# Reordering a one-core decoder layer: a key search shifted by a fifth, and a few sums and stores moved in the MLP

## The chip, the cores and the metric

The kernel runs on one core of one Trainium2 chip. The metric is device time in microseconds (us), and lower is better. A run is one execution; the profile is of one execution more, taken by the hardware profiler.

## The reference

The layer works on x of 1024 rows by 1024 columns in float32. What the change touches is the sparse attention's choice of keys and the MLP:

```python
# sparse attention: for every query, the 256 best causal keys by an indexer's score
score = einsum(relu(q_idx . k_idx), w_idx) * idx_scale      # per query, per key
score = where(key_pos <= query_pos, score, -inf)
_, sel = top_k(score, 256)                                   # ties: the lower key first
...                                                          # 8 heads attend over sel only
# differential attention: 4 heads, softmax(q1 k1) - lambda * softmax(q2 k2), all causal keys
# x = x + rmsnorm(concat(o_A, o_B) @ W_out)
# MLP
u = relu(rmsnorm(x) @ w_up)              # 1024 -> 4096
y = (u * u) @ w_down                     # 4096 -> 1024
x = x + rmsnorm(y)
```

## The kernel before, in words

Rows are handled in blocks of 128. All large products run in float32 halves: each operand is split into a high part (ScalarE copies it rounded) and a low part (VectorE subtracts), and three products stand for one.

**The search.** Blocks 0 and 1 need no choice. For blocks 2 to 7 the kernel finds each query's threshold bit by bit: `topk_round` counts how many scores lie under a trial threshold, 31 rounds, one bit each. The six blocks form two halves, `TBS = ((3, 5, 6), (2, 4, 7))`; in each round the first block of a half is counted on VectorE, the two others on ScalarE, GpSimd compares, and VectorE sets the bit (L535). `seq(gr)` lists a half's steps: a start, 31 rounds, an end, and then for each block `topk_mask1` and `topk_mask2`, which turn the score into an additive mask with a prefix sum over ties (a scan). That makes 39 steps a half and 78 in all. `topk_mask1` takes two tiles from the three buffers with the tag `pt`: `te` (signs and ties) and `tu` (the scan's result). The transposed probabilities of the differential attention, `pthl`, live in the same three buffers. The steps of both halves are merged one to one into `steps`.

**The differential attention** runs 32 units (head, block) and, between their groups, calls `run_steps(share)`, which issues the steps up to that share of the list, and pieces of the remaining projections (`dense`). Here a planner with its own cost estimates puts the instructions of every engine in order. After it, the sparse attention goes through (head, pair of blocks); its units need the masks, the pair (2, 3) first, then (4, 5), then (6, 7). There TensorE's order is written by hand, with the output projection of the other heads as filler.

**The MLP** has the order of all engines written by hand: `do(t, fn)` files a step under a due time, and all steps are issued in order of these times, so that each engine, and SyncE's DMA queue, gets its instructions in that order. The up projection makes 16 passes p of seven products of 12 matmuls (`P1`, `P6`, `P7`, `P5`, `P2`, `P4`, `P3`; a Strassen-like scheme). A pass p needs weights split in four pieces, `w1` to `w4`, of which `w2` and `w3` come from four sums of raw weights (the tile `su`, L1033 to L1036). Products land in PSUM banks, and some banks are used twice: `P7` fills bank `c`, VectorE adds it to `e2` (this is `e3`, L1273), and only then may `P4` go on in `c`. In the same way `a22` (L1279) reads bank `d` ahead of `P3`. The results are written out by `store`: ScalarE rounds (L1296), VectorE subtracts (L1300), four DMAs write to `u_d` (L1302).

The names `U0` and `D0` are due times: in `U0` the first pass starts its second product, at `D0` the down projection starts. The down projection works in units of 42 matmuls (L1427); unit n reads its left operand from `u_d` by two loads (`down_left`, L1421). In a unit, the first product's bank `a` is copied out by ScalarE (L1458) and used again by the fourth product. The raw down weights come by loads at L997, and pairs of them are subtracted on VectorE (`t13`: L1392, L1393) ahead of a split (`wd_y`).

Of the kernel before, what the change touches and what calls it, by code (L numbers as in the profile page):

```python
# [11 lines left out]
F32 = mybir.dt.float32  # L12
# [4 lines left out]
ALU = mybir.AluOpType  # L17
# [4 lines left out]
P = 128  # L22
D = 1024
S = 1024
# [9 lines left out]
MASK = 2.0 ** 100  # L34
# [16 lines left out]
def hybrid_block(ctx, tc, a):  # L51
    nc = tc.nc
    V, A, G, T = nc.vector, nc.scalar, nc.gpsimd, nc.tensor
# [12 lines left out]
    at = ats.enter_context(tc.tile_pool(name="at", bufs=1, side="right"))  # L66
# [264 lines left out]
    for kt in range(KT):  # L331
# [7 lines left out]
        g = g_preT[:, kt:kt + 1]  # L339
# [4 lines left out]
        elif kt % 3 == 0:  # L344
            n = min(3, KT - kt)
# [112 lines left out]
    score = {}  # L458
# [33 lines left out]
    NT = len(TBS[0])  # L492
# [58 lines left out]
    def topk_mask1(gr, j):  # L551
        i = TBS[gr][j]
        n = (i + 1) * P
        sc, thr = score[i], vbits[gr][:, j:j + 1].bitcast(F32)
        se = at.tile([P, 2, S], BF16, tag="pt", bufs=3, name="te")
        s_, e_ = se[:, 0, :n], se[:, 1, :n]
        u_ = at.tile([P, S], F32, tag="pt", bufs=3, name="tu")[:, :n]
        f = cnt("fm")
        A.activation(s_, sc, AF.Sign, bias=thr, scale=-1.0, accum_out=f[:, 0:1])
        V.tensor_scalar(e_, s_, 0.0, None, op0=ALU.is_equal)  # L560
        V.tensor_tensor_scan(u_, e_, e_, 0.0, op0=ALU.add, op1=ALU.max)

        V.tensor_scalar(f[:, 1:2], u_[:, n - 1:], 0.5, TOPK - n / 2, op0=ALU.mult, op1=ALU.add)
        V.scalar_tensor_tensor(f[:, 2:3], f[:, 0:1], 0.5, f[:, 1:2], op0=ALU.mult, op1=ALU.add)
        mk[i] = s_, e_, u_, f

    def topk_mask2(gr, j):
        i = TBS[gr][j]
        n = (i + 1) * P
        s_, e_, u_, f = mk[i]  # L570

        V.scalar_tensor_tensor(u_, s_, 4.0 * S, u_, op0=ALU.mult, op1=ALU.add)
        V.tensor_scalar(score[i], u_, f[:, 2:3], MASK, op0=ALU.is_gt, op1=ALU.mult)

    def seq(gr):
        r = [lambda: topk_start(gr)]
# [12 lines left out]
            idx_unit(i, h0, 1.5)  # L589
    while dense.run:  # L590
        dense.part()
    steps = []
    for k in range(len(seqs[1])):
        steps += seqs[0][k:k + 1] + seqs[1][k:k + 1]

    while dense.left() > after0:
        with tc.issue_after(anchor0[-1].ins):
# [365 lines left out]
    def do(t, fn, *args):  # L963
        todo.append((t, len(todo), fn, args))
# [52 lines left out]
    def up_weights(p, t):  # L1017

        b = wbox[p]
        do(t["ra"], lambda: b.update(ra=raw(a["wu"][2 * p])))  # L1020
        do(t["rb"], lambda: b.update(rb=raw(a["wu"][2 * p + 1])))

        def s_tile():
            if p == 0:
                b["s"] = my.tile([P, 4, 512], F32, tag="su", bufs=1, name="su0")
            else:
                b["s"] = big("hp", [P, 4, 512], "su", F32)

        s = lambda i: b["s"][:, i, :]
        ra = lambda i: b["ra"][:, i * 512:(i + 1) * 512]  # L1030
        rb = lambda i: b["rb"][:, i * 512:(i + 1) * 512]
        do(t["s"], s_tile)
        do(t["s"], lambda: V.tensor_add(s(2), rb(0), rb(1)))  # L1033
        do(t["s"] + 0.01, lambda: V.tensor_sub(s(1), ra(0), rb(0)))
        do(t["s"] + 0.02, lambda: V.tensor_sub(s(0), s(2), ra(0)))  # L1035
        do(t.get("s4", t["s"] + 0.03), lambda: V.tensor_sub(s(3), ra(1), s(0)))  # L1036
        split_at(*t["w1"], b, "w1", whl, lambda: b["ra"])
        split_at(*t["w2"], b, "w2", whl, lambda: b["s"][:, 0:2, :].rearrange("p a b -> p (a b)"))
        split_at(*t["w3"], b, "w3", whl, lambda: b["s"][:, 2:4, :].rearrange("p a b -> p (a b)"))
        split_at(*t["w4"], b, "w4", lambda: wp.tile([P, 2, 512], F32R, tag="g", bufs=1, name="w_a22"), lambda: rb(1))  # L1040
# [153 lines left out]
    U0 = E + 13.0  # L1194
# [29 lines left out]
    def mlp_up(p):  # L1224
        b = ubox[p]
        plain = p // 2 == NCH - 1
        evt = lambda nm: late["up"].tile([P, 512], F32, tag=nm, bufs=1, name=nm)

        def prod(k, o, l, h, first, last):
            do(start[p, k], lambda: up_mm(b[o], p, l, h, first, last))  # L1230

        def ab():
            ab_ = psS("pab")
            b["a"], b["b"] = ab_[:, 0, :], ab_[:, 1, :]

        def c():
            b["c"] = psM("pc")

        def d():
            b["d"] = psM("pd")  # L1240

        do(start[p, "P1"], ab)
        prod("P1", "a", "A11", "B11", True, False)
        prod("P6", "b", "S2", "T2", True, True)
        do(start[p, "P7"], c)
        prod("P7", "c", "S3", "T3", True, False)
        do(start[p, "P5"], d)
        prod("P5", "d", "S1", "T1", True, False)
        prod("P2", "a", "A12", "B21", False, True)
        prod("P3", "d", "S4", "B22", False, True)  # L1250
        prod("P4", "c", "A22", "T4", False, True)

        def u1():
            b["u1"] = late["up"].tile([P, 2, 512], F32, tag="u1", bufs=1, name="u1")

        def u2():
            b["u2"] = late["up"].tile([P, 2, 512], F32, tag="u2", bufs=1, name="u2")


        a11, a12 = (lambda i=i: b["u1"][:, i, :] for i in range(2))  # L1260
        a22, a21 = (lambda i=i: b["u2"][:, i, :] for i in range(2))

        def e1():
            b["e1"] = sp.tile([P, 512], F32, tag="e1", bufs=2, name="e1")
            A.activation(b["e1"], b["a"], AF.Copy)

        def e2():
            b["e2"] = evt("e2")
            V.tensor_add(b["e2"], b["b"], b["e1"])

        def e3():
            b["e3"] = evt("e3")
            V.tensor_add(b["e3"], b["c"], b["e2"])  # L1273

        do(end[p, "P1"] + 0.01, e1)
        do(end[p, "P6"] + 0.02, e2)
        do(end[p, "P7"] + 0.02, e3)
        do(end[p, "P5"], u2)
        do(end[p, "P5"] + 0.02, lambda: V.tensor_add(a22(), b["d"], b["e3"]))  # L1279
        do(end[p, "P5"] + 0.7, lambda: relu2(a22(), a22()))  # L1280
        t11 = max(end[p, "P2"] + 1.05, OPEN + 6.2 if p == 0 else end[p - 1, "P3"] + 3.5)
        do(t11, u1)
        do(t11 + 0.01, lambda: relu2(a11(), b["a"]))
        do(end[p, "P3"] + 0.02, lambda: V.tensor_add(a21(), b["d"], b["e2"]))
        final = p == NP - 1
        do(end[p, "P3"] + (2.9 if final else 1.2), lambda: relu2(a21(), a21()))
        do(end[p, "P4"] + 0.02, lambda: V.tensor_add(a12(), b["c"], b["e2"]))
        do(end[p, "P4"] + (4.2 if final else 0.65), lambda: relu2(a12(), a12()))
        z = end[p, "P3"]

        def store(src, g, th, tl):

            def hi():
                n = src().shape[1]
                b["st", g] = big("hp", [P, 4, n, 2, P], "stg")
                A.activation(b["st", g][:, :, :, 0, :], src().rearrange("p c (q t) -> p q c t", q=4), AF.Copy)  # L1296

            def lo():
                st, n = b["st", g], src().shape[1]
                V.tensor_sub(st[:, :, :, 1, :], src().rearrange("p c (q t) -> p q c t", q=4), st[:, :, :, 0, :].bitcast(F32))  # L1300
                for q in range(4):
                    ld.dma_start(u_d[p // 2, q, :, p % 2, g:g + n], st[:, q].bitcast(F32))  # L1302

            do(th, hi)
            do(tl, lo)

        s = lambda i: b["sd"][:, i, :]
        if plain:
            store(lambda: b["u1"], 0, z + (3.0 if final else -0.85), z + (4.6 if final else 0.6))
            store(lambda: b["u2"], 2, z + (3.6 if final else 2.3), z + (4.9 if final else 3.4))  # L1310
        else:
            store(lambda: b["u1"], 0, z - 0.85, z + 0.6)
            store(lambda: b["u2"][:, 0:1, :], 6, z - 3.0, z - 2.1)

            def sd():
                b["sd"] = big("hp", [P, 4, 512], "sd", F32)
                V.tensor_add(s(0), a21(), a22())

            do(z + 2.9, sd)
            do(z + 3.0, lambda: V.tensor_sub(s(1), s(0), a11()))  # L1320
            do(z + 3.1, lambda: V.tensor_sub(s(2), a11(), a21()))
            do(z + 3.2, lambda: V.tensor_sub(s(3), a12(), s(1)))
            store(lambda: b["sd"][:, 0:2, :], 2, z + 4.2, z + 5.3)
            store(lambda: b["sd"][:, 2:4, :], 4, z + 5.3, z + 6.5)

    for p in range(NP):
        mlp_up(p)
# [2 lines left out]
                   "w3": (end[0, "P2"] + 0.1, E + 13.8), "w4": (E + 4.5, E + 16.6)})  # L1330
    up_weights(1, {"ra": 2, "rb": 24.0, "w1": (4 * M + 4.9, 4 * M + 7), "s": U0 + 7.6, "w2": (U0 + 9.5, U0 + 10.3),
                   "w3": (U0 + 10.8, U0 + 11.6), "w4": (U0 + 13.8, U0 + 14.4)})
    up_weights(2, {"ra": U0 - 5, "rb": U0 + 9, "s": U0 + 17.0, "w1": (U0 + 16.8, U0 + 18.4), "w2": (U0 + 19.3, U0 + 20.5),
                   "w3": (U0 + 24.8, U0 + 26), "w4": (U0 + 27.6, U0 + 28.5)})
    for p in range(3, NP):
        b = t0(p - 1)
# [311 lines left out]
```

## Time and profile before

| | us |
|---|---|
| runs, median of 3 (lowest to highest) | 1376.77 (1376.04 to 1378.45) |
| the profiled execution's own time | 1375.87 |
| its span in the trace | 1374.1 |

| engine | busy us | share of the span |
|---|---|---|
| TensorE matmuls (PE) | 1290.9 | 94% |
| VectorE (DVE) | 1112.7 | 81% |
| ScalarE (ACT) | 750.2 | 55% |
| GpSimd (POOL) | 381.1 | 28% |

The span and the time of the same execution differ by 1.8 us. A share is a mean over stages: the projections up to about 190 us, the differential attention with the search to about 490, the sparse attention to about 650, the output and the up projection to about 1041, the down projection to the end.

### The profile page before, as it was taken

What the parts mean: (1) busy time and instruction counts of PE and PEld (TensorE: products, weight loads), DVE (VectorE), ACT (ScalarE), POOL (GpSimd) and SP (SyncE); (2) the same over time, 40 slices, a digit from 0 to 9 for tenths busy, and PEclk for the clock granted to TensorE, in tenths of its full rate; (3) what the DMA queues carried; (4) which work ended last, traced back from release to release, by engine and by line L of the source; (5) the groups of instructions that cost most, each with busy time, mean ns of one, the idle gap of its engine ahead of it and who ended that gap; (6) DMA issues with size and microseconds to landing.
All of it is one profiled execution on the core that took longest, in us unless ns stands there. A gap on an engine that the chain in (4) does not pass through costs nothing.

```text
span 1374.1 us, 19888 instructions
## 1 busy us (share of the span) xinstructions
PE 1290.9 (94%) x6520; PEld 1086.3 (79%) x6520; DVE 1112.7 (81%) x1984; ACT 750.2 (55%) x1435; POOL 381.1 (28%) x559
## 2 busy tenths in 40 slices
PE   8999989999998789999888899999999999999997
PEld 8988878778887778887666688888887788888886
DVE  5539999999899888887798888888887488878676
ACT  5215559888994468887455567666676312112112
POOL 6366675676575343331220000000000000000012
PEclk9999999999998889999999999999999999999999
DMA  9674464456556365532751766767678676767656
GB/s 358 210 220 126 122 188 127 120 173 183 151 159 173 111 176 143 159 96 93 241 172 48 257 241 236 259 242 261 234 261 296 239 274 213 272 212 267 219 194 215
DMA packets 152263, 272.82 MB, mean 199 GB/s; under 512 B 15328, under 2 KB 83936, under 8 KB 152160
## 3 DMA queue, kind: packets, MB, share of 16 engines
q1 hardware_dynamic: 152160, 271.55, 59.9%
q8 instruction: 52, 0.85, 0.3%
q14 instruction: 51, 0.42, 0.1%
HBM read 172.40 MB, written 99.09 MB: 198 GB/s over the span
## 4 chain that ended last, share of the span: by engine, by line
PE 56%; DVE 19%; ACT 8%; issue 6%; POOL 5%; DMA 5%; SPq 1%; DVEq 0%; POOLq 0%; ACTq 0%
PE qab L1427 10%; PE pab L1050 8%; PE qc L1427 6%; PE qd L1427 6%; PE pc L1050 6%; PE pd L1050 5%; PE pj L168 3%; ACT jk L530 2%; PE v L356 2%; DVE p L627 2%; PE sa L626 2%; PE yb L895 2%; PE si L474 2%; PE oa L852 2%; PE pta L838 1%
## 5 line engine op out<-in xcount | busy, mean ns | idle before, releaser
L168 PE MATMUL pj<-hT,w_whl 128*128 128x512 f32 (+1 forms) x960 | 225.6, 384 | 3.0 <-DVE pthl L703 1.7
L168 PEld LDWEIGHTS pj<-hT,w_whl 128*128 128x128 f32 x960 | 172.4, 189 | 35.8 <-POOL hl L217 2.1
L1568 POOL TENSOR_SCALAR rs<-ss 128x1 f32<-128x1 f32 x8 | 3.9, 491 | 608.2 <-ACT jk L1556 608.2
L530 ACT ACTIVATE jk<-score,vbits 128x768 bf16<-128x768 f32 (+1 forms) x124 | 122.1, 985 | 15.6 <-DVE vbits L535 10.5
L629 ACT ACTIVATE p<-p,st 128x512 f32<-128x512 f32 (+7 forms) x108 | 84.8, 785 | 16.5 <-DVE st L627 15.1
L1050 PE MATMUL pab<-HB,w_up 128*128 128x512 f32 x384 | 92.1, 390 | 0.0
L1050 PEld LDWEIGHTS pab<-HB,w_up 128*128 128x128 f32 x384 | 72.0, 188 | 15.0
L895 PE MATMUL yb<-wo,mbhl 128*128 128x512 f32 x192 | 76.3, 430 | 1.4 <-ACT mbhl L876 1.3
L254 PE MATMUL pv_j<-w_whl,hT 128*128 128x256 f32 x576 | 72.5, 288 | 3.1 <-POOL f L532 1.4
L254 PEld LDWEIGHTS pv_j<-w_whl,hT 128*128 128x128 f32 x576 | 70.6, 196 | 5.0 <-POOL f L532 1.6
L1001 ACT ACTIVATE w_up<-su 128x1024 fp32r<-128x1024 f32 x32 | 33.6, 1052 | 62.5 <-DVE su L1035 59.8
L820 POOL TENSOR_SCALAR p<-p,st 128x128 f32<-128x128 f32 (+7 forms) x60 | 47.8, 800 | 62.4 <-DVE st L819 62.4
L476 ACT ACTIVATE rl<-si,wabs 128x512 f32<-128x512 f32 (+5 forms) x48 | 40.5, 848 | 44.2 <-PE si L474 38.4
L844 DVE TENSOR_TENSOR ptahl<-pta,ptahl 128x512 fp32r<-128x512 f32 (+2 forms) x112 | 55.3, 495 | 9.2 <-ACT ptahl L843 6.7
L843 ACT ACTIVATE ptahl<-pta 128x512 fp32r<-128x512 f32 (+2 forms) x112 | 49.0, 439 | 21.3 <-PE pta L838 17.6
L214 POOL TENSOR_TENSOR mm<-mm 128x512 f32<-128x512 f32 (+1 forms) x40 | 52.5, 1323 | 20.2 <-DVE mm L193 11.8
L480 DVE SCALAR_TENSOR_TENSOR score<-rl,wsgn,score 128x512 f32<-128x512 f32 (+5 forms) x42 | 55.0, 1319 | 3.0 <-ACT rl L476 0.3
L1088 PE MATMUL ya<-wo,mixA 128*128 128x512 f32 x192 | 50.3, 417 | 7.0 <-DVE y L1095 3.5
L852 PE MATMUL oa<-ptahl,Va 128*128 128x256 f32 x320 | 53.0, 289 | 2.6 <-DVE ptahl L844 2.4
L852 PEld LDWEIGHTS oa<-ptahl,Va 128*128 128x128 f32 x320 | 46.2, 189 | 11.2 <-DVE ptahl L844 5.3
L217 POOL TENSOR_TENSOR hl<-mm,hl 128x512 fp32r<-128x512 f32 (+1 forms) x40 | 54.0, 1357 | 0.8
L626 PE MATMUL sa<-Kd,Qd 128*128 128x512 f32 (+4 forms) x192 | 45.6, 363 | 9.0 <-DVE st L627 9.0
(252 smaller groups left out, 3430.8 us busy)
## 6 DMA issues: line engine op xcount, KB each, us to landing
ul<-u_d SPq DMA_DIRECT2D x56, 896.0 KB, 6.2
u_d<-stg SPq DMA_DIRECT2D x184, 256.0 KB, 2.8
wst<-in_wu SPq DMA_DIRECT2D x32, 512.0 KB, 4.0
wst<-in_wd SPq DMA_DIRECT2D x32, 512.0 KB, 4.6
wst<-in_wq SPq DMA_DIRECT2D x20, 512.0 KB, 4.4
xt<-in_x SPq DMA_DIRECT2D x16, 512.0 KB, 7.1
Qd<-q_d_d SPq DMA_DIRECT2D x64, 128.0 KB, 3.2
Qa<-q_a_d SPq DMA_DIRECT2D x64, 128.0 KB, 3.4
```

The costliest lines, as they stand in the source:

```text
L168: T.matmul(p[:m, :t1 - t0], wv[pw][:, kt, :m], hTs(ph, kt, t0, t1), start=(kt == 0 and j == 0), stop=(kt == KT - 1 and j == 2))
L217: G.tensor_sub(hl[:, 1, :n], o, hl[:, 0, :n].bitcast(F32))
L254: T.matmul(p[:, j2 * 256:(j2 + 1) * 256], hTs(ph, kt, tb * P, (tb + 1) * P), w[:, pw, (kt % 4) * 256:(kt % 4 + 1) * 256], start=(kt == 0 a ...
L480: last = V.scalar_tensor_tensor(sc, r[:, :n], wsgn[:, i, h:h + 1], sc, op0=ALU.mult, op1=ALU.add)
L530: A.activation(junk_b()[:, :n], score[i], AF.Sign, bias=t[:, j:j + 1].bitcast(F32), scale=-1.0, accum_out=f[:, j:j + 1])
L626: T.matmul(s[:, b, :c1 - c0], Qd[:, hl0 + part, :], K[:, c0:c1], start=(part == 0), stop=(part == 1))
L629: A.activation(p[:, :n], p[:, :n], AF.Exp, bias=nm, scale=-1.0, accum_out=l)
L844: V.tensor_sub(hl[:, 1, c0:c1], pt[:, c0:c1], hl[:, 0, c0:c1].bitcast(F32))
L852: T.matmul(o[:, :256], v[:, 2 * g2 + kk, :], hl[:, part, kk * 256:(kk + 1) * 256], start=(g2 == 0 and kk == 0 and part == 0), stop=(last a ...
L895: T.matmul(p, hl[:, pm, ct, :], wo[1][pw][ct // 2][:, ct % 2, ch * 512:(ch + 1) * 512], start=(ct == 0 and j == 0), stop=(ct == 3 and j == 2))
L1050: T.matmul(o, w[:, pw, kt, :], H[h][ph][:, kt, :], start=(first and kt == 0 and j == 0), stop=(last and kt == 3 and j == 2), skip_group_ch ...
L1427: T.matmul(o, left[j][:, l, pl, :], right[j][:, pr, :], start=(first and j == 0 and i == 0), stop=(last and j == 1 and i == 2), skip_group ...
```

## The change

Five edits, all of them of order, but for one buffer less:

- the scan writes into the score itself in place of the tile `tu`;
- the steps of the two halves are merged by keys: the first half's steps up to the masks by 0.8 each, its six mask steps by 1.1 each, the second half's by 1. So the first half's masks stand between the last rounds of the second;
- in pass 2's weights, the four sums go from U0 + 17.0 to U0 + 20.6 and the split of `w2` from U0 + 19.3 and 20.5 to U0 + 22.4 and 23.4;
- in pass 0, the low halves of two stores (with their DMAs) go from U0 + 19.04 and 20.24 to U0 + 20.74 and 22.94 (z is U0 + 13.74 there);
- a store's DMAs become a step of their own, which stays at the old time but in the last pass: there they go from D0 + 4.6 and D0 + 4.9 to D0 + 9.7.

```diff
@@ topk_mask1
         se = at.tile([P, 2, S], BF16, tag="pt", bufs=3, name="te")
         s_, e_ = se[:, 0, :n], se[:, 1, :n]
-        u_ = at.tile([P, S], F32, tag="pt", bufs=3, name="tu")[:, :n]
+        u_ = sc
@@ topk_mask2
         V.scalar_tensor_tensor(u_, s_, 4.0 * S, u_, op0=ALU.mult, op1=ALU.add)
-        V.tensor_scalar(score[i], u_, f[:, 2:3], MASK, op0=ALU.is_gt, op1=ALU.mult)
+        V.tensor_scalar(u_, u_, f[:, 2:3], MASK, op0=ALU.is_gt, op1=ALU.mult)
@@ merging the steps
-    steps = []
-    for k in range(len(seqs[1])):
-        steps += seqs[0][k:k + 1] + seqs[1][k:k + 1]
+    last0 = len(seqs[0]) - 2 * NT
+    key = [[0.8 * k if k < last0 else 0.8 * last0 + 1.1 * (k - last0) for k in range(len(seqs[0]))], range(len(seqs[1]))]
+    steps = [f for _, _, f in sorted(((key[gr][k], gr, f) for gr in range(2) for k, f in enumerate(seqs[gr])), key=lambda e: e[:2])]
@@ store in mlp_up
             def lo():
                 st, n = b["st", g], src().shape[1]
                 V.tensor_sub(st[:, :, :, 1, :], src().rearrange("p c (q t) -> p q c t", q=4), st[:, :, :, 0, :].bitcast(F32))
+
+            def out():
+                st, n = b["st", g], src().shape[1]
                 for q in range(4):
                     ld.dma_start(u_d[p // 2, q, :, p % 2, g:g + n], st[:, q].bitcast(F32))
 
             do(th, hi)
             do(tl, lo)
+            do(D0 + 9.7 if final else tl, out)
@@
-            store(lambda: b["sd"][:, 0:2, :], 2, z + 4.2, z + 5.3)
-            store(lambda: b["sd"][:, 2:4, :], 4, z + 5.3, z + 6.5)
+            store(lambda: b["sd"][:, 0:2, :], 2, z + 4.2, z + (7.0 if p == 0 else 5.3))
+            store(lambda: b["sd"][:, 2:4, :], 4, z + 5.3, z + (9.2 if p == 0 else 6.5))
@@
-    up_weights(2, {"ra": U0 - 5, "rb": U0 + 9, "s": U0 + 17.0, "w1": (U0 + 16.8, U0 + 18.4), "w2": (U0 + 19.3, U0 + 20.5),
+    up_weights(2, {"ra": U0 - 5, "rb": U0 + 9, "s": U0 + 20.6, "w1": (U0 + 16.8, U0 + 18.4), "w2": (U0 + 22.4, U0 + 23.4),
```

## Rows read from the trace of the kernel before

**Rows 1.** The page's chain that ended last, shares by engine
```profile
PE 56%; DVE 19%; ACT 8%; issue 6%; POOL 5%; DMA 5%; SPq 1%; DVEq 0%; POOLq 0%; ACTq 0%
```

**Rows 2.** Windows: stretch, busy us (instructions) by engine, TensorE clock, DMA
```profile
190.00:425.00 235.00, 218.74 (x1239) 189.80 (x1238) 217.68 (x535) 200.68 (x473) 154.79 (x266) 0.99 0.55 155
425.00:491.00 66.00, 47.09 (x316) 43.11 (x314) 58.17 (x128) 30.45 (x72) 26.19 (x27) 0.82 0.49 139
467.00:491.00 24.00, 11.71 (x63) 10.12 (x61) 21.86 (x40) 13.22 (x26) 16.55 (x12) 0.72 0.55 163
```

**Rows 3.** TensorE's waits from 425 to 491: total us, times, longest
```profile
PE od L711 <- ACT pthl L117: 7.5, 1, 7.5
```

**Rows 4.** ScalarE's timeline: start, us, instruction, idle before it and what ended it
```profile
483.53 0.60 ACT L117 ACTIVATE pthl<-ptd 128x512 fp32r<-128x512 f32 x1 [4.52 <-DVE score L573]
```

**Rows 5.** Line L535, setting a bit: durations in ns, first and last start
```profile
L535 DVE SCALAR_TENSOR_TENSOR vbits<-mi,vbits x62: 138/158/1253, 189.8 to 417.5; 128x3 int32<-128x3 int32 x62
```

**Rows 6.** The six scans, 425 to 491: busy us, mean ns, idle before
```profile
L561 DVE TENSOR_TENSOR_SCAN tu<-te 128x512 f32<-128x512 bf16 (+5 forms) x6 | 11.2, 1860 | 0.0
```

**Rows 7.** VectorE's timeline, two of the scans
```profile
436.58 1.22 DVE L561 TENSOR_TENSOR_SCAN tu<-te 128x512 f32<-128x512 bf16 x1
...
471.05 3.02 DVE L561 TENSOR_TENSOR_SCAN tu<-te 128x896 f32<-128x896 bf16 x1
```

**Rows 8.** TensorE's timeline in pass 1: P5, P4, P3
```profile
757.60 2.89 PE L1050 MATMUL pd<-HT,w_up 128*128 128x512 f32 x12
765.95 4.61 PE L1050 MATMUL pc<-HT,w_a 128*128 128x512 f32 x12 [5.46 <-DVE e L1273]
770.40 2.91 PE L1050 MATMUL pd<-HB,w_up 128*128 128x512 f32 x12
```

**Rows 9.** VectorE's timeline there: the first sum, w1's low half, e3
```profile
760.32 0.68 DVE L1033 TENSOR_TENSOR su<-wst 128x512 f32<-128x512 f32 x1
...
762.85 1.22 DVE L1004 TENSOR_TENSOR w_up<-wst,w_up 128x1024 fp32r<-128x1024 f32 x1
...
765.12 0.68 DVE L1273 TENSOR_TENSOR e<-pc,e 128x512 f32<-128x512 f32 x1
```

**Rows 10.** ScalarE's timeline there: w1's high half
```profile
757.02 1.04 ACT L1001 ACTIVATE w_up<-wst 128x1024 fp32r<-128x1024 f32 x1
```

**Rows 11.** Windows of TensorE alone: busy us, granted clock, DMA
```profile
763.00:769.00 6.00, 3.05 (x7) 0.50 0.49 184
1067.00:1073.00 6.00, 5.24 (x12) 0.50 1.01 418
```

**Rows 12.** SyncE's queue at the start of the down projection
```profile
1052.84 4.46 SPq L1302 DMA_DIRECT2D u_d<-stg  x8
...
1058.08 1.10 SPq L1421 DMA_DIRECT2D ul<-u_d  x2
...
1059.35 2.13 SPq L997 DMA_DIRECT2D wst<-in_wd  x2
```

**Rows 13.** TensorE's timeline there: ends of units 0 and 1, unit 2, unit 3
```profile
1050.37 1.65 PE L1427 MATMUL qd<-wd_x,ul 128*128 128x512 f32 x6 [0.45 <-DVE yq L1460]
...
1057.46 1.65 PE L1427 MATMUL qab<-wd_x,ul 128*128 128x512 f32 x6 [1.29 <-ACT yu L1458]
...
1061.67 1.56 PE L1427 MATMUL qd<-wd_x,ul 128*128 128x512 f32 x6
1065.55 0.96 PE L1427 MATMUL qab<-wd_b,ul 128*128 128x512 f32 x3 [2.32 <-DMA ul<-u_d]
1067.76 1.65 PE L1427 MATMUL qab<-wd_b,ul 128*128 128x512 f32 x3 [1.25 <-DMA ul<-u_d]
...
1073.81 1.54 PE L1427 MATMUL qab<-wd_x,ul 128*128 128x512 f32 x6
```

**Rows 14.** VectorE's and ScalarE's timelines there: t13, and unit 2's first copy
```profile
1069.09 0.69 DVE L1393 TENSOR_TENSOR wst<-wst 128x512 f32<-128x512 f32 x1 [6.62 <-DMA wst<-in_wd]
...
1071.73 0.60 ACT L1458 ACTIVATE yu<-qab 128x512 f32<-128x512 f32 x1
```

## The prediction

> **What bounds the kernel now.** I read the chain that ended last first: TensorE carries 56% of it and VectorE 19% [rows 1]. So TensorE is the bound over most of the span, and what can be gained lies where it stands still. Windows of 25 us over the whole span then show three such places near the edits. The first is the end of the differential attention, 425 to 491: TensorE is busy 47.09 of 66 us at a mean clock of 0.82, VectorE 58.17 of 66; ahead of it, from 190 to 425, both are nearly full (218.74 and 217.68 of 235) [rows 2]. The second is one wait in pass 1 of the up projection, where P4 starts 5.46 us late [rows 8]. The third is unit 2 of the down projection, which waits for its loads [rows 13]. In the last two the reader should follow the queue of the engine named as releaser: it was not slow, it was given the wrong instruction first.
>
> **Pass 1 of the up projection.** TensorE ends P5 at 760.49 and can go on with P4 only after e3 [rows 8]. VectorE has no gap there: from 760.32 it makes four weight sums of pass 2 (2.53 us up to 762.85), w1's low half and a store's low half (1.13 us each, half of 765.12 - 762.85), and then e3 [rows 9]. After the change the sums and that store stand behind e3. Only w1's low half stays ahead; its other half was ready at 758.06 [rows 10], so it takes the place of the first sum at 760.32. e3 follows at 761.46, and P4 0.83 us after that, as now (765.95 - 765.12): 762.29, which is 3.66 us earlier.
>
> Then something else is late: a22 reads the bank that P3 wants. Ahead of it VectorE now has e3 (0.61), the four sums (2.53) and one store (1.13), so a22 starts at about 765.73 and P3 at 766.56, where P4 would be done at 765.2 at full speed (2.89 us, as P5 took). P3 started at 770.40 [rows 8]: a gain of 3.8 us. Behind a22 come the other store and w2's low half, 1.13 each, done by about 769; P6 of pass 2 wants w2 two products after P3's start, at about 772, so both moves are covered, by some 3 us. The two stores' DMAs move by the same steps and pass no other DMA. Without a22's wait the gain would be 3.66 and the clock's loss of 1.7, 5.4.
>
> The clock: after the old wait it stood at half (0.50 of full, 1.2 in place of 2.4 GHz) from 763 to 769 [rows 11], and P4 took 4.61 us for 2.89. After a wait of 1.29 us in another place six matmuls ran at full speed (1.65 us with the start, 1057.46) [rows 13]. The new wait is 1.8 us, nearer to the short one, so I take no fall. With a fall as long as the old one P4 would end near 767.9 and P3 near 771.2, where it now ends at 773.3: gain 2.1.
>
> **The last pass's stores.** Unit 1 ends at 1063.23. Unit 2 starts at 1065.55, stops again, and reaches its fourth product at 1073.81 [rows 13]; 18 matmuls at 0.24 us (2.89 by 12) from 1063.23 would have it there at 1067.6, so 6.2 us are lost, part wait, part half clock [rows 11]. Its two loads were issued at 1058.08, because eight stores (4.46 us of issuing, from 1052.84) and one vector load stood ahead [rows 12]. Their buffers were free at 1052.02, when unit 0 ended [rows 13]. In the new order the loads (D0 + 9.67) come ahead of the stores (D0 + 9.7): issue at about 1052.1. Even with the old 9.7 us from issue to TensorE's second start (1067.76) they are there at 1061.8, before unit 1 ends. The stores that they pass are read by the last chunk alone, hundreds of us later.
>
> What is late next is a raw weight. It is issued behind the stores (1059.35) and landed at 1069.09; VectorE stood 6.62 us for it, ScalarE behind VectorE, and ScalarE's copy that frees bank a for the fourth product ended at 1072.33, 3.2 us after the landing [rows 12, 14]. It stays behind the same stores and loads, but the vector load (0.5 MB of 4.75 MB queued from 1052.84 on, by the shapes in the code) now goes out beforehand, while the queue waits for stores. 16.25 us by 4.25/4.75 is 14.5: landing near 1066.6, bank a free near 1069.8, the fourth product near 1070.0 in place of 1073.81. Gain 3.8 us, with a stop of some 2.4 us in mid-unit. The bounds: 6.2 if nothing stops, nothing if the weight lands as late as now (the stop is then 5 us, and the clock falls).
>
> The Trainium skill, DMA: Bandwidth & Descriptors, section Queues, rings and completion order, says that each DMA engine takes its descriptors in ring order. By that the loads profit in full from being issued first, and the weight keeps its place behind stores and loads; the trace agrees as far as it goes, since the loads issued behind the stores were the ones that came late.
>
> **The search.** No instruction goes away but the second tile. In the old order the twelve mask steps are the last of the list and run from about 436 [rows 7] to past 483 [rows 4]; their six scans alone take 11.2 us of VectorE [rows 6]. `te` and `tu` leave one buffer of three for `pthl`, and it shows: ScalarE waits 4.52 us for a mask's last step to free one [rows 4], and TensorE 7.5 us behind it [rows 3]. That wait should go. But VectorE's work stays the same, and from 467 to 491 it is busy 21.86 of 24 us [rows 2]: most of TensorE's 18.9 idle us there are VectorE's queue under another name. The first half's masks move into a stretch where VectorE is full too, and six rounds of the second half move back in exchange. So the gain is bounded above by VectorE's idle time, 66 - 58.17 = 7.8 us, and a little for shorter scans; below, nothing excludes a loss, since a planner lays out the order anew. I take half of the idle time, 4 us.
>
> **Sum.** 3.8 + 3.8 + 4 = 11.6 us off the profiled execution's 1375.87 gives 1364.3. The median of the runs is 0.9 above that execution: 1365.2.
>
> **Rivals.**
>
> *The search gives nothing:* VectorE is the bound from 190 to 491, and order doesn't change its work. For it: 21.86 of 24 us busy. Against it: the 7.5 us wait for one buffer. 7.6 us remain: 1369.2.
>
> *Scans beside GpSimd:* a scan of 512 takes 1.22 us, one of 896 took 3.02 with GpSimd at work, where length alone gives 2.13: 1.42 times as long [rows 7]. From 190 to 425 GpSimd is busy 66%, after 425 40% [rows 2]. If the three scans moved forward (512, 768 and 896 columns, 5.2 us by length) stretch by 0.42, VectorE gets 2.2 us more and the search gives 1.8: 1367.4. The Trainium skill's SBUF — State Buffer, section Who interferes with whom, says that a VectorE instruction with two SBUF inputs contends with a GpSimd one that reads SBUF; the 3.02 us agrees.
>
> *The clock falls at both MLP waits:* the first gives 2.1, the second about 0.8: 6.9 with the search, 1369.9. The wait of 2.4 us speaks for it, the wait of 1.29 us against.
>
> *The tail closes:* the search gives 9, the down projection 5: 17.8, so 1359.
>
> *Slower: the second half's search ends too late.* Its last bit goes back by six steps of 3.67 us (62 rounds from 189.8 to 417.5 [rows 5]), by 22 us to about 440, and its blocks 2, 4 and 7 are all needed by the first sparse units. Now 73.5 us lie between the last bit and 491. If that stays so, the sparse attention starts 22 us late: 1391. It decides once the search loses more than 7.6 us, when the end and six masks take over 59 us. They are half of the present work, so some 37 us are likelier.
>
> *The change doesn't do what it says:* e3 or the loads wait for another buffer, and 1376 to 1377 stays.
>
> **How the numbers follow.** Chances: forecast (1361 to 1367) 0.47, search gives nothing 0.16, clock 0.12, tail closes 0.12, scans 0.06, slower 0.05, no effect 0.02. From 1357 to 1373 no more than 2 in 10 is left out; it reaches to the case in which the tail closes and past the two near 1370. A measurement here tells 0.2%, 2.75 us, from no change: faster means under 1374.0. Faster 0.87; same 0.08 (no effect, and mixtures of the weak cases); slower 0.05.
>
> **What would show it.** In pass 1: e3 right behind w1's low half, P4 some 1.8 us behind P5, a second small wait on a22. In the down projection: the loads on SyncE ahead of eight stores at about 1052 (less the gains so far), no wait on them in unit 2, a wait on ScalarE's copy in mid-unit. At the end of the search: `pthl` no longer released by a mask step, three masks between rounds, three at the end, and the first long run of the filler starting some 4 us ahead of 491. I am wrong if `pthl` is freed sooner and TensorE then waits for VectorE just as long, or if the last bit of the second half comes after 455.

## The result, and the profile after

| | us |
|---|---|
| predicted, with range | 1365.2 (1357 to 1373) |
| after, median of 5 runs (lowest to highest) | 1366.99 (1365.61 to 1371.43) |
| before, 5 runs on the same chip | 1376.77 |
| ratio | 0.9933, interval 0.992 to 0.9945: 9.2 us less |
| the changed kernel timed once more, 6 runs | 1370.39, ratio 0.9953, interval 0.9937 to 0.9969: 6.5 us less |

The profiled execution of after is the slowest of its five: 1371.43 us, with a span of 1369.6. Both timings are faster by more than 0.2%, and both intervals leave out the 11.6 us of the sum, though the first comes to within 0.6.

**Pass 1.** TensorE's timeline of after: P5, P4, P3.

```profile
755.50 2.89 PE L1051 MATMUL pd<-HT,w_up 128*128 128x512 f32 x12
760.20 2.98 PE L1051 MATMUL pc<-HT,w_a 128*128 128x512 f32 x12 [1.81 <-DVE e L1274]
764.38 3.06 PE L1051 MATMUL pd<-HB,w_up 128*128 128x512 f32 x12 [1.19 <-DVE u L1280]
```

VectorE's timeline there: w1's low half, e3, the four sums, a store, a22.

```profile
758.24 1.22 DVE L1005 TENSOR_TENSOR w_up<-wst,w_up 128x1024 fp32r<-128x1024 f32 x1
759.37 0.68 DVE L1274 TENSOR_TENSOR e<-pc,e 128x512 f32<-128x512 f32 x1
759.97 0.68 DVE L1034 TENSOR_TENSOR su<-wst 128x512 f32<-128x512 f32 x1
...
762.50 1.22 DVE L1301 TENSOR_TENSOR stg<-sd,stg 128x1024 fp32r<-128x1024 f32 x1
763.64 0.68 DVE L1280 TENSOR_TENSOR u<-pd,e 128x512 f32<-128x512 f32 x1
```

e3 stands right behind w1's low half. P4 waits 1.81 us where it waited 5.46 [rows 8], and takes 2.98 us for 4.61, so the clock did not fall. A second wait, 1.19 us on a22, stands at P3. From P5's start to P3's start it is now 8.88 us; it was 12.80 [rows 8].

**The down projection.** SyncE's queue of after, at units 1 and 2.

```profile
1045.49 1.01 SPq L1426 DMA_DIRECT2D ul<-u_d  x2
1046.97 8.86 SPq L1306 DMA_DIRECT2D u_d<-stg  x8
1056.21 1.01 SPq L998 DMA_DIRECT2D wst<-in_wd  x2
```

TensorE's timeline before, the starts of units 0 and 3:

```profile
1041.46 1.56 PE L1427 MATMUL qab<-wd_b,ul 128*128 128x512 f32 x6
...
1079.32 1.55 PE L1427 MATMUL qab<-wd_b,ul 128*128 128x512 f32 x6
```

TensorE's timeline of after: units 0, 2 and 3 begin with `wd_b`, and `wd_x` is the fourth product.

```profile
1035.56 1.52 PE L1432 MATMUL qab<-wd_b,ul 128*128 128x512 f32 x6
...
1057.18 1.55 PE L1432 MATMUL qab<-wd_b,ul 128*128 128x512 f32 x6
1065.28 2.93 PE L1432 MATMUL qab<-wd_x,ul 128*128 128x512 f32 x6 [3.78 <-ACT yu L1463]
...
1073.32 1.55 PE L1432 MATMUL qab<-wd_b,ul 128*128 128x512 f32 x6
```

VectorE's timeline of after has the wait of `t13`.

```profile
1061.99 0.69 DVE L1398 TENSOR_TENSOR wst<-wst 128x512 f32<-128x512 f32 x1 [5.40 <-DMA wst<-in_wd]
```

A window of after around the fourth product, with the columns of [rows 2]:

```profile
1064.00:1070.00 6.00, 4.72 (x11) 3.75 (x12) 1.72 (x2) 1.72 (x4) 0.00 (x0) 0.50 0.25 106
```

The loads go ahead of the stores, and unit 2 starts without a wait. But it stops in the middle for 3.78 us, and then the granted clock is 0.50 for six microseconds. Counted from unit 0's start, the fourth product comes after 29.7 us, 2.6 earlier than before (1041.46 to 1073.81). Unit 3 comes after 37.8 us, and it did after 37.9 before (1079.32). What the loads gained was lost at half clock within the same unit: from the fourth product to unit 3 it takes 8.0 us in place of 5.5.

**The end of the search.** Windows of after, over the stretches of [rows 2].

```profile
425.00:491.00 66.00, 48.31 (x326) 44.84 (x325) 56.32 (x129) 35.86 (x87) 33.90 (x38) 0.84 0.56 164
467.00:491.00 24.00, 10.21 (x42) 8.26 (x41) 19.35 (x38) 10.82 (x25) 13.91 (x15) 0.72 0.76 236
```

VectorE is busy 56.32 of the 66 us in place of 58.17, and TensorE 48.31 in place of 47.09. The line that sets a bit, in after: durations in ns, first and last start.

```profile
L535 DVE SCALAR_TENSOR_TENSOR vbits<-mi,vbits x62: 134/160/1257, 187.2 to 448.2; 128x3 int32<-128x3 int32 x62
```

TensorE's longest waits of after from 425 to 495: total us, times, longest.

```profile
PE ptb L875 <- DVE ptahl L845: 8.5, 1, 8.5
PE sa L627 <- DVE st L628: 3.3, 2, 2.7
PE yb L896 <- ACT mbhl L877: 2.8, 1, 2.8
```

The wait for `pthl` [rows 3] is gone, and the last bit is set 31 us later than before [rows 5]. In the place of the 7.5 us stands a wait of 8.5 us at `ptb`, the product that transposes `mb`, the stored results of the differential attention. The profile names `ptahl` as its releaser, but that was done at 482.85. SyncE's queue shows what came last:

```profile
472.70 0.36 SPq L265 DMA_DIRECT2D v_a_d<-vt  x1
...
478.32 0.81 SPq L872 DMA_DIRECT2D mb<-mb_d  x2
```

The first load of `mb` took 4.8 us to land, so it was there at 483.1, and `ptb` starts at 483.41. In all eleven traces with a changed search `ptb` starts 0.1 to 0.3 us after this landing, whichever instruction is named.

TensorE's timelines at the start of the filler (`yb`), before and after:

```profile
491.09 1.28 PE L895 MATMUL yb<-wo,mbhl 128*128 128x512 f32 x3 [1.31 <-ACT mbhl L876]
487.27 1.65 PE L896 MATMUL yb<-wo,mbhl 128*128 128x512 f32 x3 [2.77 <-ACT mbhl L877]
```

The last matmul of the filler starts at 647.7 in place of 649.9. One pair of traces can't price this. Of the 3.8 us at the start, 2.6 were there at the first set bit already (187.2 and 189.8). So count from the first set bit. The three traces with the old search have the filler's first matmul after 301.3 to 303.6 us and its last after 460.1 to 462.5. The six with the new search have 297.1 to 300.3 and 457.6 to 460.8. By the means the filler starts 4.0 us earlier and ends 2.0 us earlier. A part of the difference is the clock: TensorE's windows at the filler's start, before and after, have 23 matmuls and 15 in four microseconds. The columns are busy us (instructions), granted clock and DMA.

```profile
491.00:495.00 4.00, 3.86 (x23) 1.00 1.03 320
487.00:491.00 4.00, 3.73 (x15) 0.60 0.27 81
```

### The profile page after: what moved, and what is told of

Same layout as the page of the kernel before. It is cut to its first block, busy times and chain, and to the rows that moved or that the text cites. A ratio compares the mean times of both kernels' runs of the same rounds, so it can differ in the third digit from the quotient of the medians.

```text
span 1369.6 us, 19871 instructions
## 1 busy us (share of the span) xinstructions
PE 1291.1 (94%) x6520; PEld 1087.1 (79%) x6520; DVE 1110.4 (81%) x1984; ACT 750.5 (55%) x1435; POOL 385.7 (28%) x559
## 4 chain that ended last, share of the span: by engine, by line
PE 63%; DVE 15%; DMA 6%; ACT 6%; issue 4%; POOL 4%; SPq 0%; DVEq 0%; POOLq 0%; ACTq 0%
PE qab L1432 9%; PE pab L1051 8%; PE pj L168 7%; PE qd L1432 6%; PE qc L1432 6%; PE pd L1051 5%; PE pc L1051 5%; PE sa L627 3%; PE pv_j L254 2%; PE v L356 2%; PE yb L896 2%; PE si L474 2%; PE oa L853 2%; PE od L712 1%; DVE p L628 1%
```

## The experiments

Each ran in five rounds beside the kernel before on the same chip; ratios are to that kernel. "us less" is the ratio's distance from 1, times about 1376.5, and differs somewhat from the distance of the medians.

**One part alone.** Pass 1: the sums, `w2` and the two low halves of pass 0 at their new times, all else as before.

```diff
-            store(lambda: b["sd"][:, 0:2, :], 2, z + 4.2, z + 5.3)
-            store(lambda: b["sd"][:, 2:4, :], 4, z + 5.3, z + 6.5)
+            store(lambda: b["sd"][:, 0:2, :], 2, z + 4.2, z + (7.0 if p == 0 else 5.3))
+            store(lambda: b["sd"][:, 2:4, :], 4, z + 5.3, z + (9.2 if p == 0 else 6.5))
...
-"s": U0 + 17.0, ... "w2": (U0 + 19.3, U0 + 20.5)
+"s": U0 + 20.6, ... "w2": (U0 + 22.4, U0 + 23.4)
```

> Only the pass-1 edit (the four weight sums, w2's split and the two low halves of stores behind e3); search and last stores as before. Theory (VectorE's queue order alone made P4 late): 3.8 us shorter than before, ratio 0.9972; P4 starts 1.8 us behind P5's end at full clock, P3 waits some 1.2 us for a22, and from pass 2 on the distance stays. Rival (the old loss was mostly the half clock, and the new waits of 1.8 and 1.2 us bring it too): 2 us or less, and the clock at 0.50 after P4's start.

Measured: 1370.38 us, ratio 0.9956 (0.9939 to 0.9973), 6.1 us less (3.7 to 8.4). TensorE's timeline has the same two waits as the full change.

```profile
761.00 2.98 PE L1050 MATMUL pc<-HT,w_a 128*128 128x512 f32 x12 [1.80 <-DVE e L1273]
765.17 3.03 PE L1050 MATMUL pd<-HB,w_up 128*128 128x512 f32 x12 [1.19 <-DVE u L1279]
```

From pass 0's second product (the first on `pab<-HT`) to the first matmul of the down projection the trace shows 308.2 us before, and 304.4 here and in the full change: 3.8 us less. The stretch is steady: the six traces with these due times have 304.3 or 304.4, the six without the edit 308.0 to 309.3. The interval of the runs just takes in 3.8; the other 2.3 us of the 6.1 have no place in this stretch.

The last pass's stores alone:

```diff
+            def out():
...
+            do(D0 + 9.7 if final else tl, out)
```

> Only the last pass's eight stores behind the two loads of unit 2. Theory (the loads are freed at once, and the raw weight behind the stores is late next): no wait for loads, a wait of 2.4 to 4 us for ScalarE's copy at unit 2's fourth product; 3.8 us shorter if the clock holds, next to nothing if it falls, so a mean between 0 and 3.8 that differs by execution. Rival (the loads were the whole loss): 6.2 us shorter in every execution and no wait in unit 2.

Measured: 1377.06 us, ratio 1.0001 (0.9989 to 1.0013). TensorE's timeline of it, unit 2's fourth product:

```profile
1070.93 2.89 PE L1431 MATMUL qab<-wd_x,ul 128*128 128x512 f32 x6 [2.65 <-ACT yu L1462]
```

A wait of 2.65 us, near the predicted 2.4, was enough for matmuls at half clock (2.89 us for six). This execution gained 2 us from unit 0 to unit 3; the runs show none. Over the whole stage, from unit 0 to the last unit, the five traces with the stores at D0 + 9.7 have 279.8 to 282.4 us, and the six with the old order 280.1 to 282.1.

Both edits of the search alone (scan in place, merge by keys):

```diff
-        u_ = at.tile([P, S], F32, tag="pt", bufs=3, name="tu")[:, :n]
+        u_ = sc
...
+    key = [[0.8 * k if k < last0 else 0.8 * last0 + 1.1 * (k - last0) ...
```

> Only the two search edits (scan in place, keys). Theory (VectorE's queue bounds the end of the search, and a part of its idle time closes): the long run of the output projection's matmuls starts 3 to 5 us ahead of 491, and the whole is 2 to 5 us shorter. Rival 1 (the search gives nothing, the gain of the full change is the MLP's): within 1 us of before. Rival 2 (the gain grows later, in the sparse attention): more than 5 us shorter, while the filler starts less than 4 us earlier.

Measured: 1373.35 us, ratio 0.9978 (0.9965 to 0.999), 3.0 us less (1.4 to 4.8). Behind a wait of 10.0 us at `ptb` the filler starts 298.2 us after the first set bit, and its last matmul 458.6, which is 3.1 and 1.5 us less than before. The three parts alone add to 9.0 us less, the full change was 9.2 and 6.5: no sign of an interaction between them.

**Each edit of the search by itself.** The scan in place with the old order, then the keys with the tile `tu` kept.

> Only the scan in place (one buffer of pt more for the transposed probabilities); the halves' steps one to one as before. Theory A (the buffer made the end of the search late): most of the 3 us that both search edits gave, the 7.5 us wait for a transposed tile gone. Theory B (VectorE's queue is the bound, and the keys spread its work): within 1 us of before, and the wait comes back under VectorE's name.

> Only the merging by keys, the scan in a tile of its own as before. Theory A (the buffer): within 1 us of before or slower, since the first half's masks now take two buffers of three in the middle of the attention too. Theory B (the keys spread VectorE's work): 2 to 4 us shorter than before, as both search edits were.

Measured: in place 1382.2 us, ratio 1.0034 (1.0023 to 1.0045), 4.7 us *more*; keys 1378.36, ratio 1.0015 (1.0005 to 1.0025), 2.1 us *more*. Neither edit gains alone, and the two together do. With the scan in place the wait for `pthl` is gone as well, and TensorE's timeline shows what stands in its place:

```profile
491.55 1.09 PE L874 MATMUL ptb<-ident,mb 128*128 128x128 f32 x4 [12.55 <-DMA mb<-mb_d]
```

`mb` is loaded from `mb_d`, where the differential attention's last results (`ot`) are stored. SyncE's queue of this run has the loads behind two stores:

```profile
482.19 0.38 SPq L265 DMA_DIRECT2D v_a_d<-vt  x1
486.68 0.79 SPq L741 DMA_DIRECT2D mb_d<-ot  x2
488.82 4.17 SPq L871 DMA_DIRECT2D mb<-mb_d  x3
```

The chain that ended last, followed back from 494, names the first of them, the store of the last projected values (`vt`):

```profile
482.19 6.62 DMA v_a_d<-vt
488.82 2.60 DMA mb<-mb_d
491.55 1.10 PE ptb L874 x4
```

By the code that is a matter of memory: `mb` lies in the pool `p2`, which is opened in the place of `p1`, the pool of `vt`, so the load waits until `vt` is read out. VectorE's timeline shows why the store is late:

```profile
478.24 3.44 DVE L137 TENSOR_TENSOR wo<-wst,wo 128x512 fp32r<-128x512 f32 x2
...
481.60 0.47 DVE L232 SCALAR_TENSOR_TENSOR vt<-pv_j,r_pre,vt 128x256 fp32r<-128x256 f32 x1
```

So the filler's start is set by a chain that has no mask in it: the low half of the last `vt`, behind a pair of the output projection's low halves, then its store, the store's landing, the load, the transpose. VectorE made that half at 476.44 before and at 472.20 in the full change, where the store goes out at 472.70. Before, this chain was hidden: the load had landed at 484.1, and TensorE came to `ptb` only at 488.4, held up by the wait for `pthl`. No run moved the store of `vt` by itself.

With the keys alone, TensorE's longest waits from 400 to 495 begin with this one:

```profile
PE sa L627 <- DVE st L628: 8.3, 4, 3.4
```

There the filler starts early, at 485.8, but ends at 651.0: the longest of the `sa` waits, 3.4 us at 491.9, lies already in the sparse attention. A wait of 3.58 us for `pthl` (at 411.99 in the full change) is in both, so the second tile isn't its reason; two waits of 2.9 and 2.8 us, released by `fm` and by VectorE's `pthl`, are longer here. That the buffers cause this was not tried.

**Is VectorE's queue the bound of the search's end?** The changed kernel with four low halves of the output projection on GpSimd, which frees 6.2 us of VectorE behind 465:

```diff
-    ..., hi_act, (V, (V, G)[ct % 2])[half], **raw_in)
+    ..., hi_act, (V, G)[half], **raw_in)
```

> The changed kernel, with the output projection's four low halves of the second half of rows all on GpSimd; two pairs of them now stand in VectorE's queue at 465.48 (2.87 us) and 476.77 (3.36 us). Theory A, VectorE's queue sets the end of the search: 6.2 us leave it, GpSimd has room (13.91 of 24 us busy), the filler starts 3 to 5 us ahead of 487.3, and after a part is given back the median falls by 1 to 3 us. Theory B, the order that the planner makes sets it (which load or copy stands last in which queue): GpSimd takes 3.4 to 4.5 us for such a pair, the p products behind it on GpSimd come later, the filler starts at 487 or later, and the median stays within 1.5 us or rises.

Measured: 1369.22 us, ratio 0.9947 (0.9931 to 0.9963), not to be told from the changed kernel. The wait at `ptb` is still there, on `mb` now:

```profile
483.03 1.09 PE L875 MATMUL ptb<-ident,mb 128*128 128x128 f32 x4 [12.02 <-DMA mb<-mb_d]
```

VectorE is busy 16.22 us from 467 to 491 in place of 19.35, and the time of the kernel stays. The filler starts at 484.9 in place of 487.3, but that shows nothing: the six traces with the unedited new search have it between 484.8 and 488.4. So less work in VectorE's queue brought no gain that these runs can show. The same edit on the slow version with the scan in place:

> The kernel before with the scan in place, as in the run that was 4.7 us slower, and besides with the output projection's four low halves of the second half of rows on GpSimd. In that run the last pair of them (3.44 us from 478.24) stood in VectorE's queue ahead of the last differential results, whose store and loads back (mb) came last before the filler at 493.4. Theory A, that pair delays the chain of the last results: it comes 2 to 4 us earlier, the filler starts at 489.5 to 491.5, and the median falls back to 1376 to 1379.5. Theory B, the loads of mb come late by their place in SyncE's queue whatever VectorE does: the filler stays within 1 us of 493.4 and the median at 1380.5 to 1384.

Measured: 1380.13 us, ratio 1.0019 (1.0009 to 1.003). The filler starts at 491.8, 1.6 us earlier (1.0 counted from the first set bit), between the two theories and within what traces of one code differ by. The interval overlaps that of the scan in place alone, so the runs show no sure gain either. What the rows do settle is which chain it is. SyncE's queue of this run:

```profile
480.12 0.60 SPq L265 DMA_DIRECT2D v_a_d<-vt  x1
...
486.54 0.80 SPq L871 DMA_DIRECT2D mb<-mb_d  x2
488.61 0.80 SPq L741 DMA_DIRECT2D mb_d<-ot  x2
```

SyncE's waits have the releaser of the load:

```profile
SPq L871 <- DMA v_a_d<-vt: 3.8, 1, 3.8
```

The last results (`ot`) can't be what `ptb` waits for: their store goes out behind the first two loads of `mb`. The low half of `vt` comes 4.4 us earlier on VectorE (477.18), its store only 2.1 us earlier, because it stands behind loads in SyncE's queue, and it lands at 486.52, just ahead of the load. So theory A had the right pair of instructions and the wrong chain.

**How far ahead.** The changed kernel with keys of 0.9, a tenth ahead:

```diff
-    key = [[0.8 * k if k < last0 else 0.8 * last0 + 1.1 * (k - last0) ...
+    key = [[0.9 * k if k < last0 else 0.9 * last0 + 1.1 * (k - last0) ...
```

> The changed kernel, with the first half's steps merged by keys of 0.9 in place of 0.8, so that it runs a tenth ahead. Theory A, what counts is how far the masks stand from the end: the gain lies between that of the scan in place without keys (5 us slower than before in this stage) and that of the full change, so the median is 2 to 4 us above the changed kernel's. Theory B, each order is an arrangement of its own, and the end depends on what stands last in SyncE's and VectorE's queues: the median can lie on either side of the changed kernel's by up to 5 us, and the last wait of TensorE ahead of the filler has another releaser than in the changed kernel.

Measured: 1369.37 us, ratio 0.9946 (0.9929 to 0.9962). It lies between the changed kernel's two timings, and the filler starts at 485.5; the wait at `ptb` is 13.3 us and ends 0.2 us after the landing of `mb`. The releaser that the profile names, the store `mb_d<-ot`, is another than in the changed kernel, as theory B had it. That the gain grows with the distance of the masks from the end is not borne out: half the shift gives as much, though a loss of some 2 us isn't excluded.

**The raw weight first.** The changed kernel, with the last stores 1.3 us of due time later, so that one of the two weight loads of unit 2 passes them:

```diff
-            do(D0 + 9.7 if final else tl, out)
+            do(D0 + 11.0 if final else tl, out)
```

> The changed kernel with the last pass's stores at D0 + 11.0 in place of D0 + 9.7, so that the raw weight of D0 + 10.8 is issued ahead of them too. Theory (that weight is what stops unit 2 in the changed kernel): no wait on ScalarE's copy in unit 2, no fall of the clock there, and 3 to 6 us shorter than the changed kernel, most where the clock fell; some 13 us shorter than the kernel before. Rival (the weight is late by its buffer or by bytes already queued, not by its place behind the stores): within 1 us of the changed kernel, VectorE still stands over 4 us for it.

Measured: 1366.73 us, ratio 0.9917 (0.9896 to 0.9938), 11.4 us less than before (the medians are 9.6 apart). The interval overlaps both of the changed kernel's, so the gain over that kernel is read from the trace. SyncE's queue of this run:

```profile
1054.51 0.33 SPq L998 DMA_DIRECT2D wst<-in_wd  x1
1054.90 5.65 SPq L1306 DMA_DIRECT2D u_d<-stg  x8
1060.64 0.48 SPq L998 DMA_DIRECT2D wst<-in_wd  x1
```

TensorE's timeline of it, the fourth product of unit 2:

```profile
1063.86 1.67 PE L1432 MATMUL qab<-wd_x,ul 128*128 128x512 f32 x6 [1.26 <-ACT yu L1463]
```

TensorE's window of it there:

```profile
1062.00:1068.00 6.00, 4.74 (x21) 3.58 (x20) 2.34 (x3) 2.89 (x6) 0.00 (x0) 1.00 1.00 368
```

The stop is 1.26 us, where the theory had none, and the clock stays at 1.00. The first weight load is issued 17.9 us after unit 0's start, no earlier than before, but with the stores behind it `t13` can start 4.2 us after that issue, in place of 9.7. From unit 0 to unit 3 it takes 32.9 us, 4.9 less than after the change. Later waits take a part of it back (0.7 us for `ul`, 1.3 on `yu`): from unit 0 to the last unit it is 278.4 us, with 281.0 before and 282.4 and 281.5 in the changed kernel's two profiles, so 3 to 4 us of the 4.9 are left.

**Both waits.** The same, and the four sums of pass 2 and the first store's low half behind a22:

```diff
-            ... z + (7.0 if p == 0 else 5.3)) ... z + (9.2 if p == 0 else 6.5))
+            ... z + (8.5 if p == 0 else 5.3)) ... z + (10.0 if p == 0 else 6.5))
-                   "s": U0 + 20.6
+                   "s": U0 + 22.05
```

> The changed kernel with the last pass's stores behind the raw weight (D0 + 11.0), and in pass 1 the four sums and the first low half behind a22 too (U0 + 22.05 and 22.24). Theory: P3 in pass 1 waits no longer (1.2 us), unit 2 has no wait over 1.5 us and keeps full clock; 2 to 5 us shorter than the changed kernel of the same call. Rival (w2's low half or a buffer is late next, by as much): no shorter than the changed kernel with the stores behind the weight alone.

> The version with the weight's load ahead of the last stores and all four sums behind a22, once more. If its 13 us are real: median 1361 to 1366, ratio 0.988 to 0.993, and in the profile no half clock at the start of the down projection, with TensorE's only waits there at 1.3 us each. If they came from the scatter of the executions: near the changed kernel's two medians, 1367 to 1370.4.

Measured: 1363.47 us, ratio 0.9905 (0.9888 to 0.9921), and again 1364.93, ratio 0.9913 (0.9897 to 0.9929): 13.1 and 12.0 us less than before, 3 to 7 us more than the changed kernel's two gains. The first ran beside the changed kernel's second timing, and the medians are 6.9 us apart. The traces agree: pass 1's stretch takes 303.3 us in place of 304.4, and unit 0 to the last unit 276.4 and 276.7. TensorE's timeline of pass 1, where the wait on a22 is gone, and of unit 3's start:

```profile
758.29 2.98 PE L1051 MATMUL pc<-HT,w_a 128*128 128x512 f32 x12 [1.78 <-DVE e L1274]
761.11 2.88 PE L1051 MATMUL pd<-HB,w_up 128*128 128x512 f32 x12
...
1065.49 1.76 PE L1432 MATMUL qab<-wd_b,ul 128*128 128x512 f32 x6
```

This version beats both the kernel before and the changed one.

The changed kernel was timed once more beside it:

> The changed kernel once more, beside the others of this call. 9.8 us shorter than before (0.9933) as the first time. Whether its unit 2 loses time to the half clock again: theory (the wait of 3 to 4 us is at the edge, so it goes by execution) a spread of some 4 us between executions, rival (it always falls) a spread like that of the kernel before.

Its 1370.39 us are in the table above; unit 2 again waits 3.8 us and goes on at half clock, and unit 3 starts 38.3 us after unit 0.

## Why the prediction came out as it did

**The sum.** 11.6 us were predicted; 9.2 and 6.5 were measured. The time lies in the range, near the forecast, but that proves little: the range holds the rivals at 1369.2 and 1369.9 too, and the second timing is nearer to those. One of the three terms was nothing. What the experiments leave, 3.8 in pass 1 and 3.0 in the search, makes 6.8, near the second timing; that the first came to within 1.8 us of the forecast was in part luck.

**Pass 1: right, with its working.** Predicted 3.8 us, a wait of 1.8 us at P4 and a second one on a22, no fall of the clock; 3.8 us, 1.81, 1.19 and matmuls at full speed. The choice between the ends (the nearer of two waits decides about the clock) held here; it was a choice, and no rule was shown by it.

**The last stores: the mechanism right, the size wrong.** Predicted 3.8 us, measured 0 alone (0.9989 to 1.0013). The order of the queue, the unit without a wait for loads and the stop on ScalarE's copy came as said. Two steps failed. First, the weight: 14.5 us were taken from the issue of the two loads to its landing, because the vector load was gone from the queue; it took 16.5 (1045.49 to 1061.99), as long as the 16.25 with the vector load. The eight stores took 8.86 us to issue and not 4.46 [rows 12], so the weight was issued 2.8 us *later* (20.65 us after unit 0's start in place of 17.89). It landed 5.8 us after its issue in place of 9.7, so `t13` could start 1.2 us earlier (26.43 us in place of 27.63) and not 2.5. What slowed the stores was not tried. Second, the clock: the stop was 3.78 us and not 2.4, and the sum put the half clock behind it at nothing. That cost 2.5 of the 2.6 us gained at the fourth product, and even the 2.65 us of the run with this part alone brought it. The lower bound came true, by the clock, though the weight did land earlier. With one weight load ahead of the stores the stage gives 4.9 us up to unit 3 and 3 to 5 us in all. That is the same mechanism as the change's, carried one transfer further.

**The search: the size near, the reason wrong.** Predicted 4 us, measured 3.0 (1.4 to 4.8). The term stood on the 7.5 us wait for a `pthl` buffer, bounded by VectorE's idle time. With the buffers freed alone that wait vanished and the kernel became 4.7 us slower. The prediction had written that it would be wrong if `pthl` came sooner and TensorE waited for VectorE just as long. TensorE waited as long, 8.5 us at `ptb`, but for a load of `mb`, which hangs on the landing of the last `vt` store. The prediction had no such chain. It took the sum of VectorE's work for what stands behind the buffer, but 6.2 us less of it gained nothing that the runs show; in VectorE's queue the place of one instruction, the low half of the last `vt`, is what the chain hangs on. Its 18.9 idle us of TensorE are those of 425 to 491; from 467 to 491, of which the sentence speaks, they are 12.3 [rows 2]. It also had no loss at half clock at the filler's start. Where the last `vt` and its store stand explains the versions shown, by their rows; what makes the planner put them there was not tried, and stays open.

**The rivals.** *Scans beside GpSimd* falls: the six scans take 9.7 us in all in place of 11.2 [rows 6], and the one of 896 columns 2.02 in place of 3.02 [rows 7]. In their new place GpSimd was the one held up: its compare of three columns inside a round (L534, 0.26 us in the median) took 1.58 us beside the scan of 768 columns and 2.04 beside that of 896, and ended with it. *Search ends too late* falls: the last bit is at 448.2, later than the 440 worked out, and under the 455 from which it was to count. *The clock falls at both waits* was half right: at the second, not the first. *The search gives nothing* is outside the interval, just. *The tail closes* and *the change doesn't do what it says* did not come.

## What to carry to other kernels

When a load is put ahead of stores in a queue, work out what is queued behind them too, and follow it to TensorE: moving the next transfer past the stores as well turned a gain of nothing into three to five microseconds. Taking away a wait named in a profile gains only as far as the next thing behind it is earlier; take the wait away alone, on the chip, before an edit is credited with it. When the profile names a releaser that was done long before, look for a transfer that landed just then. Compare stretches from a common event and over several traces: the start of one stage differed by 3.6 us between six traces of the same code. Where a planner lays the order out anew, each edit brings a new arrangement, so two edits are to be timed together and one by one.

## What was not expected of the hardware

The same eight stores took 4.46 us to issue before, 8.86 and 8.80 after, 7.47 in the run with that part alone and 5.43 to 5.65 behind one weight load. The cause was not measured. On the clock: at this place in the kernel single waits of 1.25 to 1.3 us left it at 1.00, and those of 2.65 and 3.78 us were followed by 0.50, for matmuls of the same kind. In the kernel before, a wait of 2.32 us and, after three matmuls, another of 1.25 were followed by 0.50 [rows 11, 13]. In pass 1 one of 1.81 us left it full. The changed kernel's two timings, of five and six runs, have medians 3.4 us apart, more than the 0.2% that the prediction took for what a measurement can tell.
